# Four kinds of product operands turned by 32x32 blocks on VectorE and over DRAM, in place of TensorE transposes, in a twelve-stage decoder kernel on one core

## The chip, the core and the metric

The kernel runs on one core of a Trainium2 chip. The core has a matrix engine (TensorE, PE in the profile), a vector engine (VectorE, DVE), an activation engine (ScalarE, ACT), a general engine (GpSimd, POOL) and a queue of transfers that SyncE (SP) issues, which 16 DMA engines carry out. Each engine works through its own row of instructions in order; between engines there are only semaphores. The metric is the device time of one execution in microseconds (us), the median of several runs. The kernel before takes 2641.5 us (three runs, 2641.03 to 2641.89).

## What is computed

Two blocks, one behind the other, in float32, on 256 rows of 1024 features. The first has two layers of a mixer (two attentions and a short convolution), an attention to a memory and an MLP with a squared ReLU, each closed by a layer norm. The second has four layers: a mixer (retention in layers 0 and 3, dilated attention in 1, a gated MLP, gMLP, in 2), a SwiGLU feed-forward network (FFN, 2816 hidden features) and a gated embedding. Cut to the places that the change touches:

```
# first block
h = jnp.square(jax.nn.relu(x @ w1));  x = layer_norm(ALPHA * x + h @ w2)
# retention, per head
y = y * lax.rsqrt(mean(y * y) + EPS);  mix = (jax.nn.silu(g) * y) @ w_out
# gMLP
mix = (u * (einsum('gnm,bcmgd->bcngd', w_s * causal, vn) + b_s)) @ w_out
# FFN
gate, up = split(h @ w_in, 2);  f = (jax.nn.silu(gate) * up) @ w_out
```

In each of these four the left operand of the last product is computed with rows on the partitions, and the product needs it with features on the partitions: it has to be turned.

## The kernel before

The 256 rows are two row tiles of 128, t = 0 and 1. `thread(t)` is a Python generator that takes one row tile through the whole network and yields the name of the weight block that it wants next. The main loop goes through the blocks in the order of a plan: it starts loads (`load`, six blocks ahead, on SP's queue), cuts blocks (`split`, one ahead), gives block n to tile 0 and an earlier one to tile 1, as many blocks behind as `LAGS` says (4 for ff1, 3 for ff2, 5 for the FFN's fg and fu, 4 for fo, 1 for most of retention, 2 by default). So the two tiles are a few blocks apart and their instructions alternate. The order on each engine is then settled by a scheduler of the tile framework.

A block is 512 KB of weights, two pieces of 128x512. Products are made in three passes of reduced precision: `split` cuts a piece into a high part `wh` (a cast or scaled copy on ACT) and a low part `wl` (a subtraction on DVE). Raw blocks have 5 buffers (`RBUFS`), each kind of part 14 (`WBUFS`), seven blocks. Operands are cut the same way into a `Parts` bank (`part`), and `mm3` multiplies high by high, high by low and low by high: L318, PE's main line. `proj` computes 512 output features from a row tile in 24 such products into a PSUM bank `pj`, `outproj` accumulates the last product of a stage in two banks `acc`.

Four stages make a source of 128x512 (rows by features) piece by piece and multiply it one piece later:

- `mlp`: `ffr`, the ReLU of a ff1 product (L819), 8 pieces per layer and tile; ff2 multiplies it. Its square is taken on the way, on ACT (L825).
- `swiglu`: `ffu`, gate by up (L1103), 6 pieces per layer and tile, the last of 256 features; fo multiplies it.
- `retention`: `ro` (L914), 4 pieces per layer and tile.
- `gmlp`: `gor` (L1074), 4 pieces per tile.

Each source is turned by `transpose4`: up to four 128x128 PE transposes (L271, products with an identity) into a PSUM bank (`ffp`, `rop`, `gop`). `cut` then makes the parts from that bank: ACT the high one (L276), DVE the low one (L307). The whole turn is put on a list by `defer` and emitted by `flush`, which runs behind the products of every weight block.

Of the kernel before, what the change touches and what calls it, by code (L numbers as in the profile page):

```python
# [8 lines left out]
F32 = mybir.dt.float32  # L9
# [6 lines left out]
P = 128  # L16
D = 1024
# [14 lines left out]
# where the memory blocks of a layer stand: M in its mixer, (l, w) behind the norm w of layer l  # L32
# [5 lines left out]
ETB = ("ET", 2)  # L38
HI_ENG = "s"
# [6 lines left out]
def kernel(  # L46
# [15 lines left out]
    ps = ctx.enter_context(tc.tile_pool(name="ps", bufs=2, space=bass.MemoryType.PSUM))  # L62

# [4 lines left out]
    plan = []  # L68

    def colblock(key, mat, c0, n, gain=None):  # L70
        """gain: (layer, norm) of the second block whose gain scales the rows of mat"""
        v = mat.rearrange("(k p) n -> p k n", p=P)
        for i in range(4):
            plan.append((key + (i,), "w", [P, 2, n], v[:, 2 * i:2 * i + 2, c0:c0 + n],
                         gain and (gain[0], gain[1], 2 * i)))
# [111 lines left out]
    def load(limit):  # L187
        """start the loads up to weight block number limit"""
        while state["load"] < len(plan) and wnum[plan[state["load"]][0]] <= limit:
            key, tag, shape, src, _ = plan[state["load"]]  # L190
            state["load"] += 1
            nm = "_".join(str(s) for s in key)
            if tag == "w":
                t_ = wr.tile([P, 1024], F32, tag="wraw", name=nm)
                v = t_[:, :shape[1] * shape[2]].rearrange("p (k w) -> p k w", k=shape[1])
                nc.sync.dma_start(v, src)
                raws[key] = t_
            else:
                t_ = sb.tile(shape, F32, tag=tag, name=nm, bufs=BUFS[tag])
                nc.sync.dma_start(t_, src)  # L200
                tiles[key] = t_

    def split(limit):
        """cut the loaded blocks exactly into two parts of 12 significant bits"""
        while state["split"] < len(weights) and state["split"] <= limit:
            n = state["split"]
            key, tag, shape, src, gain = weights[n]
            state["split"] += 1
            m = shape[1] * shape[2]
            raw = raws.pop(key)  # L210
            he, le = HI_ENG[n % len(HI_ENG)], LO_ENG[n % len(LO_ENG)]
            step = m // 2
            tiles[key] = []
            for i in range(2):
                h_ = wp.tile([P, 512], F32R, tag="wh", name="wh")[:, :step]
                l_ = wp.tile([P, 512], F32R, tag="wl", name="wl")[:, :step]
                r_ = raw[:, i * step:(i + 1) * step]
                tiles[key].append((h_, l_))
                if gain:
                    gc = ngc[:, gain[0], gain[1], gain[2] + i:gain[2] + i + 1]  # L220
                    if he == "s":
                        S.activation(h_, r_, AF.Copy, scale=gc)  # L222
                    else:
                        V.tensor_scalar(out=h_, in0=r_, scalar1=gc, scalar2=None, op0=ALU.mult)
                    V.scalar_tensor_tensor(out=l_, in0=r_, scalar=gc, in1=h_.bitcast(F32), op0=ALU.mult,  # L225
                                           op1=ALU.subtract)
                else:
                    copy(he, h_, r_)
                    (V if le == "v" else G).tensor_tensor(out=l_, in0=r_, in1=h_.bitcast(F32), op=ALU.subtract)  # L229

# [56 lines left out]
    class Parts:  # L287
        """a transposed operand [feature, row], cut exactly into two parts; four feature tiles a bank"""
# [10 lines left out]
    def newbank(t):  # L299
        return tuple(sb.tile([P, 4, P], F32R, tag=f"h{t}", name=f"part{t}", bufs=8) for _ in range(2))  # L300

    def cut(bank, sl, src, scale=1.0, rows=slice(0, P), hi_eng="s"):
        """bank[sl] = scale * src in two parts"""
        hi, lo = bank[0][rows, sl, :], bank[1][rows, sl, :]
        if scale == 1.0:
            copy(hi_eng, hi, src)
            V.tensor_tensor(out=lo, in0=src, in1=hi.bitcast(F32), op=ALU.subtract)  # L307
        else:
            S.activation(hi, src, AF.Copy, scale=scale)
            V.scalar_tensor_tensor(out=lo, in0=src, scalar=scale, in1=hi.bitcast(F32), op0=ALU.mult,  # L310
                                   op1=ALU.subtract)

    def mm3(outs, xh, xl, ws, start, stop):
        """outs[i] += x.T @ ws[i] from the parts; low times low lies under float32's last bit"""
        n = len(outs)
        for a, b, s0, s1 in ((xh, 0, start, False), (xh, 1, False, False), (xl, 0, False, stop)):
            for i in range(n):
                T.matmul(outs[i], a, ws[i][b], start=s0, stop=s1)  # L318

    later = ([], [])  # L320
    behind = ([], [])

    def flush(t):
        """emit what was put off to behind the next products"""
        while later[t]:
            later[t].pop(0)()
        for _ in range(STEPS):
            if behind[t] and next(behind[t][0], True):
                behind[t].pop(0)
# [6 lines left out]
    def defer(t, on, fn):  # L336
        if on:
            later[t].append(fn)
        else:
            fn()  # L340

# [100 lines left out]
    def softmax_bank(t, src, nh, nkt, sums=None, maxs=None, normalise=True, e=None):  # L442
        """src: [P, nh, nk]; leaves exp(src-max) transposed as [P key, nh, nkt, P query]."""
# [30 lines left out]
    def layer_norm(t, l, which, acc, last):  # L474
        """the sum in acc is scaled by 1/ALPHA, and LN_EPS with it"""
# [42 lines left out]
    def rms_scale(t, srcs, nm):  # L518
        """1/rms of rows of D from two halves"""
# [10 lines left out]
    def prenorm(t, h):  # L530
        """transposed h and the row scale 1/rms; the gain is in the weights"""
# [17 lines left out]
    def get2(key, shape, tag, bufs=1):  # L549
        """a tile that both row tiles fill: made by the first, found by the second."""  # L550
# [19 lines left out]
    def mixer(t, l, xT):  # L570
# [7 lines left out]
        # projections for the sparse attention, and its index scores  # L578
# [30 lines left out]
        for b0 in (0, 2):  # L609
            # heads of one row group share a bank; two row groups' products alternate  # L610
# [22 lines left out]
        def six_heads(qT, kT_of, vs, bias_of, place):  # L633
            # heads of one row group share a bank; the two row groups' products alternate
            for pair in ([[0, 2, 4], [1, 3, 5]],) if t == 0 else ([[0, 2], [1, 3]], [[4], [5]]):
# [33 lines left out]
                for b, hs in enumerate(pair):  # L669
                    # the products go where the transposes were  # L670
# [41 lines left out]
        # chunked attention with relative bias  # L712
        BT = tiles[("BT", l)]

        # short convolution
# [9 lines left out]
        # the rows one and two before: moved down the partitions by DMA  # L725
# [28 lines left out]
    def memory_block(t, l, j):  # L754
        """keys or values of the memory rows of this tile"""
# [56 lines left out]
    def mlp(t, l, xT):  # L812
        acc = newacc(t)
        fT = Parts()
        for j in range(9):
            if j < 8:
# [3 lines left out]
                fT.banks.append(newbank(t))  # L820

                def turn(j=j, r_=r_):
                    pt = transpose4(t, [r_[:, i * P:(i + 1) * P] for i in range(4)], "ffp")
                    f = sb.tile([P, 4, P], F32, tag=f"tq{t}", name="ffT", bufs=2)
                    S.activation(f, pt, AF.Square, scale=IALPHA ** 0.5)  # L825
                    cut(fT.banks[j], slice(0, 4), f)

                defer(t, DEFER[3], turn)
# [10 lines left out]
    def retention(t, i, hT, rs):  # L839
# [42 lines left out]
        for h in range(5):  # L882
            if h < 4:
# [3 lines left out]
                # scores of this head, transposed: keys on partitions  # L887
# [27 lines left out]
                oT.banks.append(newbank(t))  # L915

                def turn(h=h, o=o):
                    pt = transpose4(t, [o[:, k * P:(k + 1) * P] for k in range(4)], "rop")
                    cut(oT.banks[h], slice(0, 4), pt)

                defer(t, DEFER[0], turn)
# [4 lines left out]
    def dilated(t, hT, rs):  # L926
# [39 lines left out]
        def join(hf, U, mall, sall):  # L966
            # join the three groups by their softmax denominators
# [59 lines left out]
    def gmlp(t, hT, rs):  # L1027
# [34 lines left out]
        for j in range(5):  # L1062
            if j < 4:
# [12 lines left out]
                oT.banks.append(newbank(t))  # L1076

                def turn(j=j, o=o):
                    pt = transpose4(t, [o[:, k * P:(k + 1) * P] for k in range(4)], "gop")
                    cut(oT.banks[j], slice(0, 4), pt)  # L1080

                defer(t, DEFER[1], turn)
# [4 lines left out]
    def swiglu(t, i, hT, rs):  # L1087
# [5 lines left out]
        for j in range(7):  # L1093
            if j < 6:
# [9 lines left out]
                fT.banks.append(newbank(t))  # L1104

                def turn(j=j, f=f, nkk=nkk):
                    pt = transpose4(t, [f[:, k * P:(k + 1) * P] for k in range(nkk)], "ffp")
                    cut(fT.banks[j], slice(0, nkk), pt[:, :nkk, :])

                defer(t, DEFER[2], turn)  # L1110
# [126 lines left out]
def _layout(a):  # L1237
# [10 lines left out]
    # distance of query row q to key column j of the two row tiles (previous, own)  # L1248
# [52 lines left out]
```

## Time and profile before

| | |
|---|---|
| median of 3 runs | 2641.5 us |
| span of the profiled execution | 2637.5 us |
| instructions in it | 36017 |
| weight traffic read from HBM | 445.89 MB |
| mean granted TensorE clock | 0.995 |

The profile is one execution on the chip. Its page gives for each engine the busy time and the share of the span, and groups instructions by line, engine and form. A row of a group reads: line, engine, operation, output<-inputs, partitions x elements, type, count, then busy time in all, mean ns of one, and the idle time of the engine before them with what ended it. In the timeline a row is start, duration, engine, line, operation, tiles and count, and in brackets the idle time ahead. In a list of waits a row is the waiting engine with its tile and line, what released it, and total us, number and longest. Names such as `fo_0_2_1` are weight blocks: FFN output, layer 0, piece 2, block 1. PE's row over the span in 40 slices (busy tenths), and the shares of the chain of work that ended last, by engine, read:

```profile
PE   8899999989999999999999999999999999999999
PE 27%; DVE 1%; issue 0%; ACT 0%; POOL 0%; ACTq 0%
```

### The profile page before, as it was taken

The numbers are of one execution on the slowest core, as the hardware profiler recorded it, in microseconds if no ns is written. First come the engines' busy times: TensorE is split into PE (matmuls) and PEld (weight loads), VectorE is DVE, ScalarE is ACT, GpSimd is POOL, SyncE is SP. The second block draws the span as 40 slices with busy tenths as digits, with TensorE's granted clock in tenths as the row PEclk, the third lists the DMA queues.
The fourth block names the chain that finished last, engine by engine and source line by source line (L and its number), as shares of the span: only waits on it lengthen the run. The fifth ranks groups of instructions, "written<-read, shape, count | busy, mean of one in ns | idle before, by whom it ended". The sixth has DMA issues, their size and how long they took to land. (4 is left out here: it accounts for less than half of the span.)

```text
span 2637.5 us, 36017 instructions
## 1 busy us (share of the span) xinstructions
PE 2592.8 (98%) x12700; PEld 2123.9 (81%) x12700; DVE 1757.6 (67%) x3217; ACT 1504.5 (57%) x2844; POOL 62.7 (2%) x92
## 2 busy tenths in 40 slices
PE   8899999989999999999999999999999999999999
PEld 7687888868788777888887887888788887878887
DVE  8765656866655766666766767667766667766666
ACT  6544455645445565555766666557656557655555
POOL 0000000000000000000000000000100000000000
PEclk9999999999999999999999999999999999999999
DMA  6453555445355555565654454656565655555654
GB/s 219 129 171 120 169 184 165 149 150 176 106 181 186 179 181 166 182 188 163 220 167 152 144 168 153 192 164 206 168 190 179 187 188 179 181 166 166 191 160 144
DMA packets 205853, 450.33 MB, mean 171 GB/s; under 512 B 14960, under 2 KB 38632, under 8 KB 204520
## 3 DMA queue, kind: packets, MB, share of 16 engines
q1 hardware_dynamic: 205672, 448.04, 53.6%
q8 instruction: 99, 1.62, 0.2%
q14 instruction: 82, 0.67, 0.1%
HBM read 445.89 MB, written 1.05 MB: 169 GB/s over the span
## 5 line engine op out<-in xcount | busy, mean ns | idle before, releaser
L318 PE MATMUL pj<-wh,part 128*128 128x512 f32 (+3 forms) x4480 | 1437.8, 388 | 0.6 <-ACT part L276 0.4
L318 PEld LDWEIGHTS pj<-wh,part 128*128 128x128 f32 x4480 | 833.8, 189 | 161.0 <-issue 9.1
L318 PE MATMUL pj<-wl,part 128*128 128x512 f32 (+3 forms) x2240 | 854.5, 382 | 0.5 <-DVE wl L229 0.5
L318 PE MATMUL acc<-wh,part 128*128 128x512 f32 x1920 | 584.5, 395 | 1.9 <-DVE part L310 1.9
L318 PEld LDWEIGHTS pj<-wl,part 128*128 128x128 f32 x2240 | 423.6, 189 | 72.9 <-issue 3.1
L318 PEld LDWEIGHTS acc<-wh,part 128*128 128x128 f32 x1920 | 356.3, 188 | 75.1 <-DVE part L310 3.0
L318 PE MATMUL acc<-wl,part 128*128 128x512 f32 x960 | 306.5, 393 | 0.0
L229 DVE TENSOR_TENSOR wl<-ff,wh 128x512 fp32r<-128x512 f32 x256 | 167.8, 687 | 110.4 <-ACT wh L276 110.1
L276 ACT CAST wh<-ff 128x512 fp32r<-128x512 f32 x256 | 149.2, 620 | 147.6 <-PE acc L318 95.5
L318 PEld LDWEIGHTS acc<-wl,part 128*128 128x128 f32 x960 | 180.3, 188 | 37.2 <-issue 0.3
L222 ACT ACTIVATE wh<-fg,ngc 128x512 fp32r<-128x512 f32 (+1 forms) x192 | 126.7, 687 | 144.2 <-PE pj L318 77.8
L225 DVE SCALAR_TENSOR_TENSOR wl<-fg,ngc,wh 128x512 fp32r<-128x512 f32 (+1 forms) x192 | 129.1, 705 | 109.6 <-ACT wh L222 109.4
L225 DVE SCALAR_TENSOR_TENSOR wl<-fu,ngc,wh 128x512 fp32r<-128x512 f32 (+1 forms) x192 | 128.0, 705 | 67.5 <-ACT wh L222 67.4
L222 ACT ACTIVATE wh<-fu,ngc 128x512 fp32r<-128x512 f32 (+1 forms) x192 | 124.2, 685 | 80.2 <-PE acc L318 51.6
L229 DVE TENSOR_TENSOR wl<-fo,wh 128x512 fp32r<-128x512 f32 x176 | 116.2, 689 | 35.0 <-ACT wh L276 34.3
L276 ACT CAST wh<-fo 128x512 fp32r<-128x512 f32 x176 | 103.7, 621 | 55.5 <-PE pj L318 51.9
L229 DVE TENSOR_TENSOR wl<-ro,wh 128x512 fp32r<-128x512 f32 x64 | 43.6, 691 | 37.7 <-ACT wh L276 37.7
L222 ACT ACTIVATE wh<-rv,ngc 128x512 fp32r<-128x512 f32 x64 | 45.3, 722 | 36.1 <-PE pj L318 28.8
L225 DVE SCALAR_TENSOR_TENSOR wl<-rv,ngc,wh 128x512 fp32r<-128x512 f32 x64 | 46.5, 749 | 29.0 <-ACT wh L222 29.0
L276 ACT CAST wh<-ro 128x512 fp32r<-128x512 f32 x64 | 39.6, 621 | 40.5 <-PE pj L318 35.6
L229 DVE TENSOR_TENSOR wl<-mkv,wh 128x512 fp32r<-128x512 f32 x64 | 42.6, 689 | 27.2 <-ACT wh L276 27.1
L276 ACT CAST wh<-mkv 128x512 fp32r<-128x512 f32 x64 | 37.1, 618 | 39.4 <-PE acc L318 18.5
(327 smaller groups left out, 3276.3 us busy)
## 6 DMA issues: line engine op xcount, KB each, us to landing
ff<-in_w_ff_dram SPq DMA_DIRECT2D x128, 512.0 KB, 3.6
fo<-in_ffn_out_dram SPq DMA_DIRECT2D x88, 512.0 KB, 3.6
fg<-in_ffn_in_dram SPq DMA_DIRECT2D x80, 512.0 KB, 3.5
fu<-in_ffn_in_dram SPq DMA_DIRECT2D x80, 512.0 KB, 4.4
mkv<-in_w_mkv_dram SPq DMA_DIRECT2D x32, 512.0 KB, 4.2
rv<-in_ret_in_dram SPq DMA_DIRECT2D x32, 512.0 KB, 3.8
rg<-in_ret_in_dram SPq DMA_DIRECT2D x32, 512.0 KB, 3.6
ro<-in_ret_out_dram SPq DMA_DIRECT2D x32, 512.0 KB, 3.5
```

What stands on the lines that cost most here:

```text
L222: S.activation(h_, r_, AF.Copy, scale=gc)
L225: V.scalar_tensor_tensor(out=l_, in0=r_, scalar=gc, in1=h_.bitcast(F32), op0=ALU.mult, op1=ALU.subtract)
L229: (V if le == "v" else G).tensor_tensor(out=l_, in0=r_, in1=h_.bitcast(F32), op=ALU.subtract)
L276: S.copy(o, i)
L318: T.matmul(outs[i], a, ws[i][b], start=s0, stop=s1)
```

## The change

The turns of the four sources leave PE. `turn_by_dma` first turns every 32x32 block of the source on DVE and writes the blocks, regrouped, to a tile `xt` (it shares the two buffers of the tag `ET`). Four DMAs, one per group of 32 partitions, write `xt` to a DRAM tile `xd` (four buffers per row tile) in such an order that one more DMA reads it back with features on the partitions, in runs of 512 B (256 B for the FFN's last piece). The read-back goes into the source's own tile. The high part is then copied from there by ACT and the low one made by DVE, for ff2 behind the square on ACT. The two later steps stand in a list `due` that `flush` counts down: the read-back is emitted one flush after the turn, the cuts three flushes after it. The bank of parts is taken at the cuts, not at the turn.

```diff
+XBUFS = 4
+
+BACK, CUT = 1, 3
...
     def flush(t):
         while later[t]:
             later[t].pop(0)()
+        for d in due[t]:
+            d[0] -= 1
+        while due[t] and due[t][0][0] <= 0:
+            due[t].pop(0)[1]()
...
+    def turn_by_dma(t, src, nkk, parts, j, square=None):
+        w = 32 * nkk
+        xt = sb.tile([P, 512], F32, tag=ETB[0].format(t=t), name="xt", bufs=ETB[1])[:, :4 * w]
+        V.transpose(xt.rearrange("p (q k a) -> p q k a", q=4, a=32), src.rearrange("p (k q a) -> p q k a", q=4, a=32))
+        d_ = dr.tile([4, 32, 4, P], F32, tag=f"xd{t}", name="xd")
+        dv = d_.rearrange("q a i e -> (q a i e)")[0:P * 4 * w].rearrange("(q a i e) -> q a i e", q=4, a=32, i=4)
+        for i in range(4):
+            nc.sync.dma_start(dv[:, :, i, :].rearrange("q a e -> a q e"),
+                              xt[32 * i:32 * i + 32, :].rearrange("a (q e) -> a q e", q=4))
+        z = src
+        due[t].append([BACK, lambda: nc.sync.dma_start(z, dv.rearrange("q a i e -> (q a) (i e)"))])
+        def fin():
+            bank = parts.banks[j] = newbank(t)
+            zv = z.rearrange("p (i k b) -> p k i b", i=4, k=nkk)
+            hi, lo = (x[:, 0:nkk, :].rearrange("p k (i b) -> p k i b", i=4) for x in bank)
+            if square:
+                f = sb.tile([P, 4, P], F32, tag=f"tq{t}", name="ffT", bufs=2)
+                S.activation(f[:, 0:nkk, :].rearrange("p k (i b) -> p k i b", i=4), zv, AF.Square, scale=square)
+                cut(bank, slice(0, nkk), f[:, 0:nkk, :])
+            else:
+                S.copy(hi, zv)
+                V.tensor_tensor(out=lo, in0=zv, in1=hi.bitcast(F32), op=ALU.subtract)
+        due[t].append([CUT, fin])
+        due[t].sort(key=lambda d: d[0])
...
-                fT.banks.append(newbank(t))
-
-                def turn(j=j, f=f, nkk=nkk):
-                    pt = transpose4(t, [f[:, k * P:(k + 1) * P] for k in range(nkk)], "ffp")
-                    cut(fT.banks[j], slice(0, nkk), pt[:, :nkk, :])
-
-                defer(t, DEFER[2], turn)
+                fT.banks.append(None)
+                turn_by_dma(t, f, nkk, fT, j)
```

`mlp` (with `IALPHA ** 0.5` as `square`), `retention` and `gmlp` are edited in the same way. Other turns (`transposed`, the heads' turns in the mixers) stay on PE.

How the rows of the engines move is shown at two places. The first is the middle of the first FFN, piece 3 of row tile 0. DVE, before: the source `ffu` is made, and the low part of the operand, from the PSUM bank `ffp`, stands behind two cuts of weights.

```order
L1103 SCALAR_TENSOR_TENSOR ffu_11770<-pj_11680,fsc0_10754,fth_11677 128x512
L229 TENSOR_TENSOR wl_11783<-fo_0_2_1_11661,wh_11782 128x512
L229 TENSOR_TENSOR wl_11787<-fo_0_2_1_11661,wh_11786 128x512
L307 TENSOR_TENSOR part0_11773<-ffp_11796,part0_11772 128x512
L229 TENSOR_TENSOR wl_11822<-fo_0_2_2_11687,wh_11821 128x512
```

DVE, after, from the same source on (L356 is the block transpose, L375 the low part):

```order
L1124 SCALAR_TENSOR_TENSOR ffu_11910<-pj_11816,fsc0_10876,fth_11813 128x512
L356 STREAM_TRANSPOSE xt_11912<-ffu_11910 128x512
L233 TENSOR_TENSOR wl_11928<-fo_0_2_1_11797,wh_11927 128x512
L233 TENSOR_TENSOR wl_11932<-fo_0_2_1_11797,wh_11931 128x512
L233 TENSOR_TENSOR wl_11961<-fo_0_2_2_11827,wh_11960 128x512
...
L229 SCALAR_TENSOR_TENSOR wl_12041<-fg_0_4_1_11894,ngc_92,wh_12040 128x512
L375 TENSOR_TENSOR part0_11997<-ffu_11910,part0_11996 128x512
L229 SCALAR_TENSOR_TENSOR wl_12045<-fg_0_4_1_11894,ngc_92,wh_12044 128x512
```

The low part has moved from behind two weight cuts to behind eleven other instructions, between the two halves of block fg_0_4_1. SP, after, in the same place (L200 loads weights, L360 writes to DRAM, L363 reads back; before, the row holds the loads alone):

```order
L200 DMA fo_0_2_3_11850<-in_ffn_out_dram 128x1024
L200 DMA fg_0_4_0_11872<-in_ffn_in_dram 128x2x512
L200 DMA fg_0_4_1_11894<-in_ffn_in_dram 128x2x512
L360 DMA xd_11914<-xt_11912 32x4x128 x4
L200 DMA fg_0_4_2_11925<-in_ffn_in_dram 128x2x512
L200 DMA fg_0_4_3_11958<-in_ffn_in_dram 128x2x512
L363 DMA ffu_11910<-xd_11914 128x512
L200 DMA fu_0_4_0_11980<-in_ffn_in_dram 128x2x512
```

Two weight loads stand between the writes and the read-back, which waits for the writes, and further loads behind it. ACT, after, around the high part (L374), which waits for the read-back:

```order
L280 CAST wh_11982<-fo_0_2_3_11850 128x512
L280 CAST wh_11986<-fo_0_2_3_11850 128x512
L226 ACTIVATE wh_12008<-fg_0_4_0_11872,ngc_92 128x512
L226 ACTIVATE wh_12012<-fg_0_4_0_11872,ngc_92 128x512
L226 ACTIVATE wh_12040<-fg_0_4_1_11894,ngc_92 128x512
L374 CAST part0_11996<-ffu_11910 128x512
L226 ACTIVATE wh_12044<-fg_0_4_1_11894,ngc_92 128x512
```

Before, the high part stood two blocks earlier on ACT, behind the casts of fo_0_2_1. The second place is the end of that FFN on PE, where the last and shorter piece of row tile 0 is used. Before, six products of the projection `pj` with 256 columns stand right ahead of the first use of its bank `part0_12364`:

```order
L318 MATMUL pj_12404<-wh_12330,part1_10890 128x256
L318 MATMUL pj_12404<-wl_12331,part1_10890 128x256
L318 MATMUL pj_12404<-wh_12330,part1_10891 128x256
L318 MATMUL acc0_10756<-wh_12457,part0_12364 128x512
L318 MATMUL acc1_10757<-wh_12461,part0_12364 128x512
```

After, products of row tile 1's `acc` have come to stand ahead of that use (`part0_12602`):

```order
L322 MATMUL pj_12557<-wh_12482,part1_11012 128x256
L322 MATMUL acc0_11029<-wh_12500,part1_12427 128x512
L322 MATMUL acc1_11030<-wh_12504,part1_12427 128x512
...
L322 MATMUL acc1_11030<-wh_12537,part1_12427 128x512
L322 MATMUL acc0_11029<-wl_12534,part1_12427 128x512
L322 MATMUL acc1_11030<-wl_12538,part1_12427 128x512
L322 MATMUL acc0_11029<-wh_12533,part1_12428 128x512
L322 MATMUL acc0_10878<-wh_12614,part0_12602 128x512
```

Eleven products moved ahead, so the use stands later on PE's row than before.

More of the change, by code (lines that the diff above doesn't have):

```diff
@@ L62 @@
     ps = ctx.enter_context(tc.tile_pool(name="ps", bufs=2, space=bass.MemoryType.PSUM))
+    dr = ctx.enter_context(tc.tile_pool(name="dr", bufs=XBUFS, space=bass.MemoryType.DRAM))
     tiles = {}
@@ L321 @@
     behind = ([], [])
+    due = ([], [])
     def flush(t):
@@ L819, in mlp @@
                 V.tensor_scalar(out=r_, in0=p, scalar1=0.0, scalar2=None, op0=ALU.max)
-                fT.banks.append(newbank(t))
[L822 to L828, printed above, removed]
+                fT.banks.append(None)
+                turn_by_dma(t, r_, 4, fT, j, IALPHA ** 0.5)
             if j > 0:
@@ L914, in retention @@
                 V.scalar_tensor_tensor(out=o, in0=y, scalar=rr[:, 0:1], in1=th, op0=ALU.mult, op1=ALU.mult)
[L915 to L921, printed above, removed]
+                oT.banks.append(None)
+                turn_by_dma(t, o, 4, oT, h)
             if h > 0:
@@ L1075, in gmlp @@
                                            in1=u[:, 256 * k:256 * k + 256], op0=ALU.add, op1=ALU.mult)
[L1076 to L1082, printed above, removed]
+                oT.banks.append(None)
+                turn_by_dma(t, o, 4, oT, j)
             if j > 0:
@@ L1103, in swiglu @@
                 V.scalar_tensor_tensor(out=f, in0=pu[:, :n], scalar=sc[:, 0:1], in1=th, op0=ALU.mult, op1=ALU.mult)
-                fT.banks.append(newbank(t))
-                def turn(j=j, f=f, nkk=nkk):
-                    pt = transpose4(t, [f[:, k * P:(k + 1) * P] for k in range(nkk)], "ffp")
-                    cut(fT.banks[j], slice(0, nkk), pt[:, :nkk, :])
-                defer(t, DEFER[2], turn)
+                fT.banks.append(None)
+                turn_by_dma(t, f, nkk, fT, j)
             if j > 0:
```

## The prediction

> **What bounds the kernel now.** I read the head of the page first, then the engines' busy times in three stretches where many of the turns lie (ff2, FFN, retention), then who waits for whom.
>
> ```profile
> span 2637.5 us, 36017 instructions
> PE 2592.8 (98%) x12700; PEld 2123.9 (81%) x12700; DVE 1757.6 (67%) x3217; ACT 1504.5 (57%) x2844; POOL 62.7 (2%) x92
> q1 hardware_dynamic: 205672, 448.04, 53.6%
> core 0: us, PE busy (x) PEld busy (x) DVE busy (x) ACT busy (x) POOL busy (x), PEclk, DMA share, GB/s
> 760.00:870.00 110.00, 110.00 (x504) 91.20 (x503) 62.34 (x98) 55.36 (x96) 0.00 (x0) 1.00 0.57 186
> 1110.00:1270.00 160.00, 160.00 (x773) 134.39 (x772) 101.15 (x156) 88.49 (x145) 0.00 (x0) 1.00 0.59 184
> 1655.00:1800.00 145.00, 145.00 (x701) 121.88 (x700) 90.58 (x140) 78.77 (x130) 0.00 (x0) 1.00 0.59 182
> ACT wh L222 <- PE pj L318: 253.9, 213, 3.2
> ```
>
> In all three stretches TensorE (PE) is busy for the whole time at a clock of 1.00. VectorE (DVE) is busy 57 to 63%, ScalarE (ACT) 50 to 55%, the DMA engines 57 to 59%. The last row (total, times, longest) says that ACT, which cuts the weights, waits for PE to free the buffers, not PE for ACT. So in these stages a PE instruction taken away shortens the run at once, and work added on DVE, ACT or the queue is free until PE has to wait for it. The span is 4.0 us under the median of 2641.5; I add 4.0 at the end.
>
> **What goes: 400 transposes on PE.** 32 turns of four for ff2, 40 of four and 8 of two for the FFN, 16 and 8 of four for retention and gMLP: 128 + 176 + 64 + 32.
>
> ```profile
> L271 PE MATMUL ffp<-tab,ffu 128*128 128x128 f32 x176 | 27.0, 272 | 0.0
> L271 PE MATMUL ffp<-tab,ffr 128*128 128x128 f32 x128 | 19.5, 273 | 0.0
> 768.10 0.62 PE L318 MATMUL acc<-wh,part 128*128 128x512 f32 x2
> 768.56 0.60 PE L271 MATMUL ffp<-tab,ffr 128*128 128x128 f32 x4
> 768.91 0.48 PE L318 MATMUL pj<-wh,part 128*128 128x512 f32 x1
> 769.23 0.39 PE L318 MATMUL pj<-wl,part 128*128 128x512 f32 x1
> ...
> 772.66 0.62 PE L318 MATMUL acc<-wh,part 128*128 128x512 f32 x2
> 773.11 0.39 PE L318 MATMUL pj<-wh,part 128*128 128x512 f32 x1
> 773.34 0.39 PE L318 MATMUL pj<-wl,part 128*128 128x512 f32 x1
> ```
>
> (The groups under L271 are the FFN's and ff2's: busy us and mean ns behind the bar. Of the timed rows the first column is the start, the second the duration.) One transpose lasts 272 ns, but they overlap, so the price is what they push the next product back. The same three instructions start 769.23 - 768.10 = 1.13 us apart with a turn between them and 773.34 - 772.66 = 0.68 without: 0.45 for four, 0.1125 each, 400 x 0.1125 = **45.0 us**. The groups' busy time (overlaps counted once) would give 27.0 / 176 = 0.153, 61 us in all; it counts time that the neighbours' records share, so I keep 45 and hold 61 as the far end.
>
> The Trainium skill ("TensorE: Matmul & The Clock Gate", Part 4: PE-mode transpose) gives about 275 ns for a transpose inside a kernel. The rows' 272 agree, and by that price the sum would lose 110 us; the starts 0.1125 apart say that the price is paid in latency, not in PE's time.
>
> **A wait that goes.**
>
> ```profile
> PE gop L271 <- DVE gor L1074: 3.1, 1, 3.1
> ```
>
> PE's transposes of gMLP waited 3.1 us once for their source. Without them the products behind go ahead, unless weights are late there: 0 to 3.1, I take **1.5**, the middle, as nothing in the row leans either way.
>
> **What comes in, and where it is hidden.** Per turn: one DVE transpose of 128x512, four 64 KB writes to DRAM, one 256 KB read back (half of it in the 8 short turns), and the two cuts as before, now from SBUF. The ff2 square stays.
>
> ```profile
> L868 DVE TENSOR_TENSOR rxs<-rxs,cb 128x512 f32<-128x512 f32 x16 | 11.0, 687 | 0.1
> L513 DVE TENSOR_SCALAR xf<-xTp,lnc 128x128 f32<-128x128 f32 x80 | 30.0, 406 | 0.8 <-PE xTp L512 0.6
> L196 SPq DMA_DIRECT2D ff<-in_w_ff_dram x128: 327/354/379, 211.5 to 860.0; - x128
> pr<-in_p_dram SPq DMA_DIRECT2D x8, 128.0 KB, 2.8
> fg<-in_ffn_in_dram SPq DMA_DIRECT2D x16, 256.0 KB, 2.7
> fo<-in_ffn_out_dram SPq DMA_DIRECT2D x88, 512.0 KB, 3.6
> row<-in_x_dram SPq DMA_DIRECT2D x4, 256.0 KB, 4.6
> out_dram<-x SPq DMA_DIRECT2D x4, 256.0 KB, 2.3
> DMA to landing us min/median/max: 3.3/4.6/5.9
> DMA to landing us min/median/max: 2.5/3.6/9.3
> ```
>
> The DMA rows end in the median us from issue to landing; of the last two, one is for `row`, the input rows, the other for all weight loads. No row shows the DVE transpose. A pass over SBUF tiles of that size takes 0.687 (L868); four small 128x128 passes would be 4 x 0.406 = 1.6. I take 0.69 with ends 0.41 and 1.6. It adds 104 x 0.69 = 72 us to DVE, a few per cent of a third of its time that is free: cost 0 itself (at 1.6 us still 0: 166 us against 880 idle), its delay counted in the trip below. Traffic grows by 104 x 512 KB = 53 MB on 448, about 12%, mostly in 512 B pieces; the DMA share rises from 0.57 to some 0.65 to 0.7 there, which alone stops nothing.
>
> **The trip in the steady FFN.** For row tile 0 of the first FFN:
>
> ```profile
> 1198.14 0.75 DVE L1103 SCALAR_TENSOR_TENSOR ffu<-pj,fsc,fth 128x512 f32<-128x512 f32 x1
> 1204.02 1.89 DVE L229 TENSOR_TENSOR wl<-fo,wh 128x512 fp32r<-128x512 f32 x3
> 1208.82 1.41 ACT L222 ACTIVATE wh<-fg,ngc 128x512 fp32r<-128x512 f32 x2 [1.31 <-PE pj L318]
> ...
> 1213.83 0.61 PE L318 MATMUL pj<-wh,part 128*128 128x512 f32 x2
> L276 ACT CAST part<-ffp 128x512 fp32r<-128x512 f32 (+1 forms) x48 | 26.0, 541 | 26.4 <-PE ffp L271 26.4
> ```
>
> The source is ready at 1198.9, turned by 1199.6, the fourth write issued by 1201.0 (4 x 0.354). No row shows a 64 KB write that shares the queue. Ends: 2.3 (the output's write) and 4.6 (`row`, the slowest of the small transfers); I take 3.7, the 2.8 of the 128 KB row and 0.9 for what 256 KB more cost in the queue (3.6 - 2.7). It lands at 1204.7. The order puts two weight loads ahead of the read-back, the later of which waits for the first of the three cuts at 1204.02 (done 1204.65), so SP issues the read-back near 1205.4. Ends for it: 2.7 (`fg`, the same size) and 5.9 (the slowest `row`); I take 4.5, near the median of `row`: 2.7 with a 512 KB load ahead of it in the queue (2 x 0.9). It is there at 1209.9.
>
> The new cut stands on ACT's row behind the first half of block fg_0_4_1, which ends at 1208.82 + 0.70 = 1209.5, so ACT waits 0.4 us. Queued behind it are that block's second half and later weights. PE uses the second half at 1213.83, 3.83 us after its present end at 1210.21 (the cut on ACT takes 0.54 of it, its partner on DVE as much again): 2.6 us may be lost there before PE stands still. So the FFN stalls when write and read together take over 9.5 us (mine: 8.2). The bank is used over 22 us after the source product in these 40 turns by the order; ff2's middle turns have more. SP's queue: the loads behind the read-back stand up to 4 us, while five raw buffers of 2.72 us each (1208.82 to the next block's cut at 1211.54) give 4 x 2.72 - 3.6 = 7.3. Cost **0**; PE has no idle time there to win, so nothing below zero; at the far ends, 4.6 + 5.9 = 10.5, 40 x 1.0 = 40 us.
>
> **The ends of the stages.** At the first and last ff2 turns and the last ones of retention, gMLP and FFN, 11 pairs of turns, little work stands between source and use: by the changed order, at 0.227 us a product (773.11 to 773.34), 11.6 / 13.1 us at ff2's first (tiles 0 / 1), 13.5 at its last, 12.9 for retention, 13 for gMLP, 12.3 / 10.6 for the FFN's short last turn. With landings of 2.8 and 3.6 the trip takes about 11.4 (ff2: relu 0.68, turn 0.69, issues 1.42 + 0.35, square and cuts 1.9), 12.7 (retention, whose source takes 2.6), 11 (gMLP) and 9.4 (short turn). Let x be what the two landings take beyond 2.8 + 3.6 = 6.4. With each pair paying its worse turn once (the stall of one gives time to the other): ff2 first 2(x - 0.2), ff2 last (x - 0.9) + (x - 2.0), retention 2(x - 0.1), FFN 4(x - 1.2), gMLP (x - 1.9), none below zero. My 8.2 means x = 1.8: 3.2 + 0.9 + 3.4 + 2.4 = 9.9, so **+10**. At x = 0 it is 0, at 4.1 it is 35.
>
> **Sum**: 2637.5 - 45.0 - 1.5 + 10 + 0 = 2601.0 span, and 4.0 make **2605 us**, 1.4% faster.
>
> **The rivals.**
>
> - *A longer trip, paid at the ends alone.* At x = 2.6 to 3.4 the ends cost 18 to 28 and the FFN 0 to 12: 2613 to 2634, near 2622. For it: landings of up to 9.3 in the last DMA row. Against: the median of that row is 3.6.
> - *Slower: the read-back stands in the way of the weights.* If ACT waits in order for the read-back beyond its 2.6 us in each of 40 FFN turns, the 46.5 come back. At x = 3.55 (write and read 10 us together) ends (28) and FFN (18) eat the gain; at the far end, x = 4.1, the cost is 35 + 40, or 2670 us. For it: the queue is shared with loads and 512 B pieces are new on it. Against: no 256 KB row has a median above 4.6.
> - *No change.* That the transposes stay on PE is out: its order holds 400 fewer. But the 45 us turn up as PE waiting for cuts, x near 3.4 to 3.6 or two small losses together: 2636 to 2647. PE's stages would then show idle time of that sum. Against: DVE and ACT are 37 to 50% idle there.
> - *More*: PE's price is 0.153, or the ends cost nothing with short landings: 2637.5 - 61 - 1.5 + 4 = 2579 to 2592.
>
> The Trainium skill ("VectorE: DVE Perf Modes", The three transpose paths) warns that a plain DMA copy which transposes by strides is 19 times slower than the transposing path, when the innermost stride at the target is large. By it every trip would miss its window and the slow rival would be far worse than 2670; here both ends move runs of 512 B (256 B in the short turns), the 32x32 part is done on DVE, and no run shows such a copy, so I leave it inside that rival.
>
> **How the numbers follow.** Forecast (2592 to 2613): 0.55; longer trip (2613 to 2636): 0.22; no change: 0.06; slower: 0.14; more: 0.03. The range, 2592 to 2640, holds the first two and about half of the third, 0.80. A measurement of this kernel can tell about 0.2% (5.3 us) from no change; faster by more than that: 0.55 + 0.22 + 0.03 = 0.80, within it 0.06, slower 0.14.
>
> **What would show it.** The transposes of the four sources gone from PE's groups, and the ff2, FFN and retention stretches each shorter by 0.45 per turn with PE still at full; the DVE transpose near 0.69; writes landing near 3.7 and read-backs near 4.5; the waits of ACT for the read-back short; and PE waits for the new cuts at the stage ends alone, about 10 us in all. It would be wrong if those waits are found in the middle of the FFN, if weights come late behind the read-backs, or if a DVE transpose takes several us.

## The result, and the profile after

The changed kernel takes 2621.2 us (median of 4 runs, 2616.7 to 2629.5) against 2641.3 (4 runs, 2639.8 to 2641.9): a ratio of 0.993, 95% interval 0.9914 to 0.9945. It is 20.0 us faster; forecast were 36. The time lies in the stated range, in the part that was given to the rival of a longer trip, and not in the forecast's own.

The head of the page of the changed kernel (span, busy time by engine, traffic by queue):

```profile
span 2619.8 us, 36087 instructions
PE 2554.4 (98%) x12300; PEld 2084.1 (80%) x12300; DVE 1815.6 (69%) x3321; ACT 1505.8 (57%) x2844; POOL 62.9 (2%) x92
q1 hardware_dynamic: 280552, 500.50, 62.0%
```

Three stretches out of the middles of ff2 and the FFN, by the view of windows (columns as before):

```profile
300.00:420.00 120.00, 120.00 (x538) 99.59 (x537) 76.26 (x119) 64.11 (x110) 0.00 (x0) 1.00 0.78 237
1110.00:1250.00 140.00, 140.00 (x651) 117.20 (x650) 94.45 (x148) 78.21 (x127) 0.00 (x0) 1.00 0.73 222
1650.00:1780.00 130.00, 130.00 (x604) 108.82 (x603) 85.98 (x134) 71.02 (x116) 0.00 (x0) 1.00 0.73 219
```

In the middles PE is as full as before, and the DMA share is higher than I had guessed (0.73 to 0.78). Over the span PE's busy time fell by 38.4 us and the span by 17.7, so PE stands idle 20.7 us more than before. The new operations by the view of their tile (count, ns min/median/max), the list of DMAs and the landings of the FFN's read-back (us):

```profile
L356 DVE STREAM_TRANSPOSE xt<-ffr x32: 667/705/714, 271.8 to 867.1; 128x512 f32<-128x512 f32 x32
L360 SPq DMA_DIRECT2D xd<-xt x416: 303/432/1676, 272.6 to 2572.9; - x139
xd<-xt SPq DMA_DIRECT2D x384, 64.0 KB, 2.3
DMA to landing us min/median/max: 3.0/4.5/5.5
```

And ACT's waits for the read-backs (total us, times, longest):

```profile
ACT part L374 <- DMA ffu<-xd: 25.2, 28, 1.9
ACT part L374 <- DMA ro<-xd: 21.9, 12, 3.3
ACT ffT L371 <- DMA ffr<-xd: 16.4, 21, 2.2
```

The DVE transpose takes 0.705, a write lands in 2.3, a read-back in 4.5; issuing a write costs SP 0.432. (The 512 B runs that the text on the change and the prediction give to the read-back are those of the writes; by the diff a partition's row is read back in one run of 2 KB, 1 KB in the short turns.)

Where PE waits now, at the end of the second ff2 (rows of SP, ACT and PE from the timeline) ...

```profile
867.83 1.80 SPq L360 DMA_DIRECT2D xd<-xt  x4
869.73 2.14 SPq L200 DMA_DIRECT2D rq<-in_ret_in_dram  x2
872.72 0.34 SPq L363 DMA_DIRECT2D ffr<-xd  x1
...
877.30 0.63 ACT L371 ACTIVATE ffT<-ffr 128x512 f32<-128x512 f32 x1 [1.24 <-DMA ffr<-xd]
877.96 0.62 ACT L280 CAST part<-ffT 128x512 fp32r<-128x512 f32 x1
...
875.87 0.39 PE L322 MATMUL acc<-wh,part 128*128 128x512 f32 x1
878.63 0.73 PE L322 MATMUL acc<-wh,part 128*128 128x512 f32 x2 [2.37 <-ACT part L280]
```

... the writes take SP 1.8 us, two weight loads follow, the read-back goes out 3.1 us after the last write and lands 4.6 later, the square and the cut take 1.3, and PE stands for 2.37 us. And behind the first FFN, where the embedding begins (`prp` its transposes, `pep` its products):

```profile
1266.40 0.72 PE L322 MATMUL acc<-wh,part 128*128 128x512 f32 x2
1267.91 0.44 PE L275 MATMUL prp<-tab,pr 128*128 128x128 f32 x2 [0.79 <-DVE part L311]
1269.39 0.73 PE L322 MATMUL pep<-wh,part 128*128 128x512 f32 x2 [1.04 <-ACT part L280]
1269.96 0.76 PE L322 MATMUL pep<-wl,part 128*128 128x512 f32 x2
1270.52 1.05 PE L322 MATMUL pep<-wh,part 128*128 128x512 f32 x2
1271.37 1.05 PE L322 MATMUL acc<-wh,part 128*128 128x512 f32 x2
...
1273.83 0.39 PE L322 MATMUL pep<-wh,part 128*128 128x512 f32 x1
1274.06 0.39 PE L322 MATMUL pep<-wl,part 128*128 128x512 f32 x1
```

The same place by windows:

```profile
1266.00:1270.00 4.00, 2.17 (x12) 1.40 (x12) 4.00 (x9) 3.64 (x10) 0.92 (x1) 1.00 0.90 289
1270.50:1273.50 3.00, 3.00 (x8) 2.33 (x8) 0.73 (x2) 0.00 (x0) 0.00 (x0) 0.50 0.71 243
```

No bank from DRAM is waited for here by name. PE has nothing to do between row tile 0's last product and the embedding's operand. PE is busy 2.17 of 4 us, and then runs at a granted clock of 0.50 for about 3 us: products start 0.43 us apart (1270.52 to 1271.37 is two of them), at full clock 0.23 (1273.83 to 1274.06).

To sum such places I took, from the trace of each kernel, how much later each PE product starts than is usual for its pair of forms (a form is the shape of a product; usual is the lower quartile of all such pairs). Delays of more than 0.25 us are added by place, in us. A stretch at half clock delays each product by less than that (0.43 against 0.23) and is not in the table:

```
                        before  after  ffn_end_pe  early_rows  ends_dma  ends_pe
first and last ff2         0     8.1       4.7         7.1        3.4       0
last of retention          0     3.8       3.0         2.9        4.0       0
gMLP                       3.6   2.9       2.9         2.9        3.6       2.9
first use of FFN's last    0     0         0           1.1        0.5       0
embedding                  0     9.0       0           0          5.7       0
inside the stages          6.5   8.1       7.5         7.5        6.5       8.4
elsewhere                 50.8  53.5      51.0        52.1       51.2      52.1
```

From before to after the rows add up to 24.5 us of new gaps, 20.9 of it at ff2, retention and the embedding. Each column is one execution, and small differences say little: the code of ff2 is the same in `ffn_end_pe` as in the changed kernel, and has 4.7 there against 8.1.

### The profile page after: what moved, and what is told of

The parts are those of the page before. It is cut to its first block, busy times and chain, and to the rows that moved or that the text cites. A ratio compares the mean times of both kernels' runs of the same rounds, so it can differ in the third digit from the quotient of the medians.

```text
span 2619.8 us, 36087 instructions
## 1 busy us (share of the span) xinstructions
PE 2554.4 (98%) x12300; PEld 2084.1 (80%) x12300; DVE 1815.6 (69%) x3321; ACT 1505.8 (57%) x2844; POOL 62.9 (2%) x92
## 5 line engine op out<-in xcount | busy, mean ns | idle before, releaser
L229 DVE SCALAR_TENSOR_TENSOR wl<-rv,ngc,wh 128x512 fp32r<-128x512 f32 x64 | 46.7, 747 | 24.5 <-ACT wh L226 24.3
L229 DVE SCALAR_TENSOR_TENSOR wl<-pg,ngc,wh 128x512 fp32r<-128x512 f32 x64 | 46.6, 748 | 21.4 <-ACT wh L226 20.6
```

## The experiments

Theory A: each transpose gives its 0.1125 us wherever it goes; what is lost again is lost at the stage ends, by waits there and by cover that was moved. Theory B: a turn over DRAM gives only part of its 0.45 us everywhere, since the queue, late weights or the engines take the rest. The first four kernels tell these apart. `turn_by_pe` is the turn of the kernel before, as a function.

**ends_pe**: the 22 turns at the ends go back to PE.

```diff
-                turn_by_dma(t, r_, 4, fT, j, IALPHA ** 0.5)
+                (turn_by_pe if j in (0, 7) else turn_by_dma)(t, r_, 4, fT, j, IALPHA ** 0.5)
...
-                turn_by_dma(t, o, 4, oT, h)
+                (turn_by_pe if h == 3 else turn_by_dma)(t, o, 4, oT, h)
...
-                turn_by_dma(t, o, 4, oT, j)
+                (turn_by_pe if j == 3 else turn_by_dma)(t, o, 4, oT, j)
...
-                turn_by_dma(t, f, nkk, fT, j)
+                (turn_by_pe if j == 5 else turn_by_dma)(t, f, nkk, fT, j)
```

> The 22 turns at the stage ends (ff2's pieces 0 and 7, the last piece of retention, gMLP and FFN; 72 transposes) go back to TensorE, the other 82 turns keep the trip over DRAM. Theory A (each removed transpose gives its 0.1125 us everywhere, and what the changed kernel loses again, 28 us more of PE gaps, is lost at the stage ends alone, by waits for the banks there and by the embedding behind the FFN, whose cover was moved away): 328 x 0.1125 = 36.9 us gained and no new gaps, span about 2600.6, time 2604 to 2607; the gaps at the first products of ff2, ro, go and at the embedding's transposes are gone. Rival B (a turn over DRAM gives only part of the 0.45 us wherever it stands, since queue, late weights or engines take the rest): 328 / 400 of the 20 us measured, 16 us, time about 2625.

2600.7 us (four runs within 0.2), ratio 0.9848 (0.9834 to 0.9863). 40.1 us faster than before. The gaps at ff2, retention and the embedding are gone (table); gMLP's 2.9 stay, half of them at the bank of a first piece that still goes over DRAM. A's mechanism holds, though the time is 3 us below its range; B is out by 24 us. It beats both kernels.

**ends_dma**: the reverse, `turn_by_dma` and `turn_by_pe` exchanged in those four lines.

> The reverse: only the 22 turns at the stage ends take the trip over DRAM, the other 82 stay on TensorE. Theory A: 72 x 0.1125 = 8.1 us gained and the 28 us of gaps at the ends stay, so some 20 us slower than before, 2661 (2650 to 2665). Rival B: 72 / 400 of the 20 us, 2638.

2648.9 us, ratio 1.0033 (1.002 to 1.0046): 8.1 slower. The sign is A's: with the 8.1 us that the transposes give, the ends cost 16 us. But that is less than A's 28, and the time is just below A's range. In the table the ends have 13.6 here and 20.9 in the changed kernel: they depend on their neighbours. With the second turn on PE, the first ff2 turns have no gap. In the changed kernel eight writes, of two turns, stand together there on SP, so that the second turn's go out 1.9 us after the first's:

```profile
285.52 3.75 SPq L360 DMA_DIRECT2D xd<-xt  x8
```

**ffn_end_pe**: only the FFN's last turns go back (the fourth of the four edits of `ends_pe`).

> Only the last, short turn of each FFN (8 turns, 16 transposes) goes back to TensorE, all others keep the trip. Theory A: 1.8 us of transposes come back, and the gaps of about 10 us ahead of the embedding's transposes and first products go, with the half-clock stretches behind them (3.41 us at half speed, 1.7 us each, two in the profiled run): 2621 - 11 = 2610, 2607 to 2613. Rival B': the embedding waits for something of its own (its input rows or weights come late behind the read-backs on the queue): those gaps stay, time 2621 to 2624.

2609.1 us (2605.2 to 2614.1), ratio 0.9881 (0.9866 to 0.9896). 12.1 us faster than the changed kernel with 16 more transposes. The embedding's 9.0 us of gaps are gone, as A said; the rest of the 12.1 is not taken apart.

**twice_pe**: the price of a transpose, in the kernel before.

```diff
             T.transpose(p[:, i, :], s, ident)
+            if nm in ("ffp", "rop", "gop"):
+                T.transpose(p[:, i, :], s, ident)
```

> The kernel before with each of the 400 transposes of the four sources issued twice into the same place. Theory A (PE pays 0.1125 us for each): 45 us more, 2686 (2683 to 2690). Rival by the groups' busy time (0.153): 61 us, 2702. Rival by the duration of one (0.272): 109 us, 2750.

2683.0 us, ratio 1.016 (1.0145 to 1.0176): 42.2 / 400 = 0.1055 us each, near the 0.1125 read from the timeline; the group's busy time (0.153) and a single duration (0.272) are out.

The next four ask what makes the ends dear: missing cover, SP's row, or the length of the trip.

**early_rows**: the embedding's rows are loaded, turned and cut ahead of the last fo block.

```diff
+            if j == 6:
+                embedding_rows(t, i)
             if j > 0:
                 yield from outproj(t, acc, ("fo", i, j - 1), ...
```

> The changed kernel, with the embedding's own rows loaded, turned and cut ahead of the FFN's last piece of products, not behind its norm; the same work, only earlier, so that the embedding's first products may stand on PE's row where PE waited. Theory A (the gaps of some 10 us there are missing cover: row tile 1's products, which stood between, wait for their own bank): the gaps ahead of the embedding go, with the half-clock stretches, 2621 - 11 = 2610 (2607 to 2613), as when the FFN's last turns went back to PE. Rival (PE waits there for row tile 1's trip, whatever stands between): the wait moves to the first product of the last fo block, 2618 to 2622.

2612.4 us (2608.6 to 2616.9), ratio 0.9891 (0.9875 to 0.9906): 8.9 us faster than the changed kernel, with all turns over DRAM. In the changed order the embedding's transposes stood on PE's row right behind the FFN, since the products of row tile 1 that had stood between them before waited for their own bank. With the embedding's operand ready early its first products fill that place. So the 9 us were missing cover. 1.1 us moved to the FFN's bank.

**read_pool**: the read-backs on GpSimd's queue.

```diff
-        due[t].append([BACK, lambda: nc.sync.dma_start(z, ...
+        due[t].append([BACK, lambda: nc.gpsimd.dma_start(z, ...
```

> The changed kernel, with the read-backs issued by GpSimd's queue, not SP's, all else alike. Theory Q (a read-back stands 1 to 2 us behind weight loads on SP's row, and the loads behind it): the 11 stage ends get 1 to 2 us shorter trips, some 10 us in all, 2611. Rival L (landings of 4.5 us are set by the DMA engines that the weights share, and GpSimd takes its own time to issue): no gain, 2619 to 2630, the waits of ACT for read-backs as long as before.

2688.0 us, ratio 1.0184 (1.0167 to 1.0201): 67 us slower than the changed kernel, outside both expectations. The read-backs are issued hardly sooner in ff2 (1.96 us after the last write, median, against 2.24), and there they land later: 5.7 us against 4.6 (in the FFN 4.6 against 4.5). In the middle of the first ff2 (SP, ACT and PE):

```profile
341.38 3.24 SPq L200 DMA_DIRECT2D ff<-in_w_ff_dram  x4
...
349.79 0.63 ACT L371 ACTIVATE ffT<-ffr 128x512 f32<-128x512 f32 x1 [7.48 <-DMA ffr<-xd]
...
350.98 0.50 PE L322 MATMUL pj<-wh,part 128*128 128x512 f32 x1 [1.13 <-ACT wh L280]
353.42 0.50 PE L322 MATMUL pj<-wl,part 128*128 128x512 f32 x1 [1.94 <-DVE wl L233]
```

The read-back of this piece went out on GpSimd at 343.1, amid four weight loads that SP sent right behind the writes. In the changed kernel SP sends two at the same piece, waits for the writes, sends the read-back, and only then the next loads:

```profile
334.70 2.15 SPq L200 DMA_DIRECT2D ff<-in_w_ff_dram  x2
337.03 0.34 SPq L363 DMA_DIRECT2D ffr<-xd  x1
337.86 6.74 SPq L200 DMA_DIRECT2D ff<-in_w_ff_dram  x3
```

So ACT stands 7.48 us, the weight cuts queued behind come late, and PE waits for weights in the middle of a stage: 37.9 us by the measure of the table inside the stages, where the changed kernel has 8.1, and 17.7 at the ends of ff2. The granted clock falls with the gaps: PE runs at 0.50 for 71.6 us of this execution and for 25.1 us of the changed kernel's, which at half speed is up to 23 us of the 67. This is the mechanism of the prediction's slow rival, weights that come late behind a read-back. By the rows, SP's wait for the writes, which theory Q held for a cost, kept the loads off the read-back. That was not tried apart from GpSimd, and the landings, 1.1 us longer in the median, do not by themselves give a wait of 7.48: the cause of the 67 us stays open in part.

The Trainium skill ("DMA: Bandwidth & Descriptors", Issuing engines are not separate DMA queues) says that DMAs from several engines run on the same 16 DMA engines and interleave, so that another issuer saves issue time alone. The FFN's landings, 4.6 by GpSimd and 4.5 by SP, agree; those of ff2, 5.7 and 4.6, changed with what was issued around them.

**mid_read2** and **mid_read3**: `ends_pe`, with each read-back done two or three times, one after the other.

```diff
-        due[t].append([BACK, lambda: nc.sync.dma_start(z, ...)])
+        back = lambda: [nc.sync.dma_start(z, ...) for _ in range(2)]
+        due[t].append([BACK, back])
```

> The version with PE turns at the stage ends (2600.7), its 82 other read-backs done twice, the second waiting for the first: about 4.5 + 0.4 us more of trip in the middle of the stages and nowhere else. Theory M (the margin of the prediction: the FFN's turns stall PE when write and read together take over 9.5 us; the runs show 2.3 + 4.5, so now 11.7): 40 x 2.2 = 88 us more, 2689, ff2's middle unhurt. Rival W (ACT's place in the row is not tight, since PE has more cut weights ahead than I counted): below 20 us more, 2601 to 2620.

> The same with three read-backs each, about 9.8 us more of trip. Theory M: write and read 16.6, 40 x 7.1 = 284 us from the FFN, and ff2's middle turns (24, some 7 us of slack) a few us each: 2900 to 2960. Rival W: stalls begin, 20 to 150 us more, 2620 to 2750.

2608.8 us (ratio 0.9874, 0.9859 to 0.9889) and 2627.7 (0.9949, 0.9931 to 0.9967): 8 and 27 us more than `ends_pe`. The trip of the FFN's turns grew from 10.2 to 14.0 us in the first and to 18.2 in the second. By my margin 88 and 284 us were due. The order tells why: on ACT's row the cut of piece 3, row tile 0, stands ahead of the second half of fg_0_4_1 in the changed kernel, and ahead of fg_0_4_3 in `mid_read2`. The place has moved a block and a half back with the longer trip, and by the order the bank is used over 22 us after its source in either case. So such a trip costs little as long as the cut's place goes with it. The size is rival W's in both. A longer trip with the cut held at its place was not run.

**early_ends** and **ends_pe_again**: both remedies in one, PE turns at the ends of ff2, retention and gMLP, the FFN all over DRAM with early rows; and `ends_pe` beside it on the same chip.

> Both remedies: PE turns at the ends of ff2, retention and gMLP (14 turns), the embedding's rows early, and so the FFN's last turns over DRAM again. Theory A (a turn over DRAM costs nothing where other products cover it, at the FFN's end too): 8 x 0.225 = 1.8 us less than with PE turns at all ends, 2599 (2597 to 2600.5). Rival (the FFN's last trip still leaves small waits at the first product of its bank and at the embedding): 2601 to 2604.

> The version with PE turns at all stage ends once more, on the same chip as the one beside it, for the difference of the two: 2600.7, within 0.5 us, if its 0.2 us of spread is its own and not that chip's.

2602.7 us (2601.6 to 2604.8), ratio 0.9858 (0.9841 to 0.9874), and 2601.4 (2600.0 to 2603.0), ratio 0.9852 (0.9837 to 0.9866). They cannot be told apart. The 1.8 us of A did not show, the rival's 2601 to 2604 did. The repeat misses the 0.5 us that were expected of it, and its runs lie 3 us apart, not 0.2. `ends_pe` remains the best that was run.

## Why the prediction was right in direction and half in size

**PE's 45 us**: right. Doubling the transposes cost 42.2, and `ends_pe` gains 40.1 for 328 of the 400, 0.122 each. Of the 40.1 up to 4.5 may be clock: PE ran at 0.50 for 28.6 us of the profiled execution of the kernel before and for 19.7 us of that of `ends_pe`. That was not tried by itself.

**The wait of gMLP**, 1.5: the 3.1 us went, but there PE now waits for a cut weight (1.4) and for the bank of the first piece (1.4), which the prediction did not count: a gain of 0.7 us in the table, not 1.5.

**DVE, queue, traffic**: right in the main. The transpose at 0.705 (predicted 0.69), read-backs at 4.5 (4.5); writes at 2.3, not 3.7, but issued at 0.43, not 0.354. The whole trip in the FFN, from the start of the DVE transpose to the start of the cut, is 11.0 by the prediction's times (1198.9 to 1209.9) and was measured at 10.3. The DMA share rose to 0.73 to 0.78, not 0.65 to 0.7.

**The steady FFN at 0**: right in the result. ACT waits up to 1.9 us for its read-backs and PE does not. The stated margin (a stall above 9.5 us of landings) was wrong as a law: I held the cut's place in ACT's row fixed, and in `mid_read2` the place moved with the trip. It was wrong as a sum too: from 1210.21 to 1213.83 are 3.62 us, not 3.83, and 2.6 us beyond the end of the first half, of which my 8.2 used 0.4, make 10.4.

**The ends of the stages at +10**: this is the step that failed. Measured are 8.1 for ff2 (4.1 predicted), 3.8 for retention (3.4), 0 for gMLP's last bank (0) and for the FFN's (2.4): 11.9 by waits for a bank, against 9.9. That match is luck. My formula with the measured median landings (2.3 and 4.5, x = 0.4) gives 1.0. The trips at the ends were long for other reasons, which the sum put at nothing. At the end of the second ff2 the DVE transpose starts 2.0 us after its source is done, behind a weight cut that waits for ACT and a low part (3.2 us at the first ff2's end), and the read-back goes out 3.1 us after the last write:

```profile
864.42 0.68 DVE L857 TENSOR_SCALAR ffr<-pj 128x512 f32<-128x512 f32 x1
865.88 0.69 DVE L233 TENSOR_TENSOR wl<-ff,wh 128x512 fp32r<-128x512 f32 x1 [0.78 <-ACT wh L280]
866.50 0.68 DVE L311 TENSOR_TENSOR part<-ffT,part 128x512 fp32r<-128x512 f32 x1
867.10 0.70 DVE L356 STREAM_TRANSPOSE xt<-ffr 128x512 f32<-128x512 f32 x1
```

At the first ff2's end one read-back also took 6.9 us to land. What the step left out altogether is the 9.0 us behind the FFN, more than half of the 16 us that the forecast missed, and the half clock that may follow. I saw in the order that eleven products had been moved ahead of the first use of row tile 0's last bank, and counted them as room for the trip. I did not ask where they were missing: they, and those of row tile 1 that waited for its bank, had covered the norm and the embedding's first operand. `early_rows` and `ffn_end_pe` show it: either fills or restores that place, and the 9.0 us go. A stage end has only so many independent products; what is spent ahead of a late operand is gone behind it.

**The rivals**: the longer trip at the ends (near 2622) gave nearly the time, 2621.2, but by luck: the median landings were shorter than mine, not longer, the trips at the ends were long by waits ahead of the landings, and the 9.0 us at the embedding are in no rival. Of the slow rival, `read_pool` showed the mechanism, in ff2 more than in the FFN. That its 67 us are near the price of that rival's far end (75) is chance: they lie for the greater part in ff2 and, for up to 23, in the clock, and the far end was priced by the stage ends and the FFN's 40 turns. The rival of more says 2592 where the ends cost nothing; by the prediction's own terms it is 2595.

## What to carry to other kernels

Where PE is full, moving its transposes to other engines pays their issue distance (0.11 us here), not their duration, and only where the turned operand is not needed soon: turn in the old way at the first and last piece of a stage, and over the long way in between. When a changed order moves independent work ahead of a wait, look for the place that this work covered before. And read the position of a new wait in the order of the new kernel; a scheduler shifts it, so a margin taken from the old order says little.

## What the runs showed of the hardware

PE's granted clock fell to 0.50 after less idle time than I would have thought. Before the stretch at 1270.5 PE idled 1.83 of 4 us, in pieces of 0.79 and 1.04; the kernel before has the like, with a longer gap, by its windows:

```profile
886.00:888.20 2.20, 0.33 (x2) 0.02 (x1) 2.20 (x5) 1.44 (x4) 0.00 (x0) 1.00 0.70 212
888.70:891.90 3.20, 3.20 (x11) 2.54 (x10) 3.10 (x6) 1.81 (x6) 0.37 (x1) 0.50 0.17 40
```

At the embedding of the changed kernel it fell in two of four layers in the profiled run, though the gaps are alike in all four. The clock records of the traces say where the difference lies: in each trace the stretches at 0.50 start a whole number of 3.413 us apart. Divide the changed kernel's execution into pieces of 3.413 us on that grid: in two layers both gaps fall into one piece (1.83 us idle), and the next piece is at 0.50; in the other two they fall into two pieces (0.91 and 1.04, 1.15 and 0.81), and the clock stays at 1.00. In the twelve traces, without the first and last 30 us of each, a piece at full clock with over 1.93 us idle is always followed by one at 0.50, one with under 1.53 us never, and between them both occur.

The runs of that kernel lie 13 us apart, with mean clocks of 0.991 to 0.995 (the slowest has the lowest); those of `ends_pe`, which has no gap there, 0.2 us, and 3 us in the repeat. But `ffn_end_pe` and `early_rows`, without gaps there too, spread by 9 and 8 us. That short gaps which sometimes halve the clock make the spread was not tried by itself.

The Trainium skill ("TensorE: Matmul & The Clock Gate", Why this matters for your kernels) asks for no idle gaps over some 3 us to keep the clock. The rows above differ: gaps of about 1 us, two close together, were enough.
